# Score matmuls with the low query parts on 64 partitions, and the first head's operands made earlier

## Chip, cores and metric

One core of a Trainium2 chip runs the whole kernel. The metric is the device time of one execution in microseconds; three runs were timed, and one more execution was profiled.

## What is computed

One layer of a streaming encoder step for 1024 prompt frames and 64 sample frames of width 1024: a half-step SwiGLU, one input projection into [u | q | k | v], an S5 state-space mixer with a gated output (u), differential attention with four heads (q, k, v), an output projection, cross attention into 256 memory tokens, a second half-step SwiGLU and a final norm. The part that the change touches is the attention of the prompt, all in float32:

```python
s = einsum('bqhme,bkhme->bhmqk', q, k) * 64 ** -0.5     # two maps m of 64 dims per head
s = s - slope[h] * abs(qpos - kpos)                     # masked by chunks of 64
p = softmax(s)
w = p[:, :, 0] - lam * p[:, :, 1]
out = einsum('bhqk,bkhv->bqhv', w, v)
```

and, ahead of it, the gate of the state-space mixer, `y * sigmoid(y @ w_glu + b_glu)`.

## The kernel before

The whole step is written as one stream of Python that emits instructions; a scheduler of the framework orders the instructions of each engine by readiness and by their place in the program, gives out buffers and sets the waits. Rows of 128 x 1088 float32 come from one pool of 36 buffers (`row()`), PSUM banks from a pool of seven (`bank()`).

Float32 precision is had from the fast float32r form by splitting an operand x into a rounded high part and a low part x - high. A full product takes three matmuls (high x high, high x low, low x high), done by `mm3` (line 176) for the projections.

**The gating units** (lines 1683 to 1697). Four units f, one for each 128 columns of `w_glu`. `unit` (from line 190) issues 36 matmuls with `mm3`, ScalarE takes the sigmoid from PSUM (L1693), VectorE multiplies with y (L1695), and the product is stored to memory (L1697). It is loaded again at steps 32 to 35 of the attention loop (`Y_AT`). Before the matmuls of the last unit (f == 3) head 0 is set up: `head_start(0)` and `q_stack(heads[0], 6)`.

**Operands of a head.** `head_start` (line 1461) makes two key tiles `ks[m]` of 128 x 1024, one for each map m. The 64 partitions of map m (`hi_`) hold the high part of the keys, cast by ScalarE (L1471); the other 64 (`lo_`) hold the low part, made by GpSimd (L1472). It also loads the bias of the head on SP (L1474). `q_stack` (line 1481) does the same for 256 queries at a time, for both maps, in a tile [128, map, r, 256]: r = 0 holds the high part of the queries in both halves of the partitions (ScalarE L1488, GpSimd L1489), so that one matmul over 128 partitions with `ks[m]` gives q_high k_high + q_high k_low. r = 1 holds the low part of the queries in the half `hi_` (GpSimd L1490) and zeros in the other half (GpSimd L1491), so that a second matmul over 128 partitions adds q_low k_high.

**The attention loop** (from line 1708). 32 blocks of 128 queries, four heads with eight blocks each, in the order 7, 6, ..., 0 (`ORDER`); block i sees (i + 1) x 128 keys. Step n does the scores of block n, `combine` of block n - 2, `transposes` of block n - 4 and `values` of block n - 5 (`LAGS`). `scores` issues, for each map and each cut of the keys (one cut up to 512 keys, else two), the two matmuls at L1508 into one bank; VectorE adds the bias and takes the minimum out of PSUM (L1511), ScalarE takes the exponential (L1517). `combine` is VectorE work (L1525 to L1528), `transposes` go through TensorE (L138) and ScalarE (L1538), `values` are float32 matmuls (L1544, each in two records). At step 1 of each head `stream` adds the attention of the 64 sample frames into the cache as background work (its scores L1579, its values L1614, and two matmuls over 64 partitions, L1615). `q_ready(n + 2)` makes a query tile two steps ahead, and `head_start` of the next head is called at step 5 of a head (`HEAD_AT`). After the loop the memory projection follows (matmuls at L1761), whose weights are loaded and split in advance (L145, L162, L163).

The two matmuls for one bank, as they stand before:

```python
for r in range(2):
    T.matmul(p[:, :c1 - c0], s.qs[i // 2][:, m, r, (i % 2) * P:(i % 2 + 1) * P], s.ks[m][:, c0:c1],
             start=(r == 0), stop=(r == 1))
```

Of the kernel before, what the change touches and what calls it, by code (L numbers as in the profile page):

```python
# [10 lines left out]
F32 = mybir.dt.float32  # L11
# [6 lines left out]
P = 128  # L18
# [21 lines left out]
ORDER = (7, 6, 5, 4, 3, 2, 1, 0)  # L40
# [29 lines left out]
def tile_hymba_step(ctx: ExitStack, tc: tile.TileContext, a, o):  # L70
# [15 lines left out]
    V, A, G, T = nc.vector, nc.scalar, nc.gpsimd, nc.tensor  # L86
# [8 lines left out]
    def row(shape=(P, NT), dt=F32):  # L95
        return rows.tile(list(shape), dt, tag="r", name=nm("r"))

    def bank():
        return ps.tile([P, 512], F32, tag="b", name=nm("b"))

    def small(shape, tag, dt=F32):
        return sp.tile(list(shape), dt, tag=tag, name=nm(tag), bufs=6 if tag in ("rr", "ss", "mn", "xr") else 3)
# [89 lines left out]
    def unit(wsrc, xs, mid=None, chs=CHS):  # L192
        return units([wsrc], xs, mid, len(xs) // 2, chs)[0]

    def chunks(p, t):

        return [(pc[:, :c1 - c0], t[:, c0:c1]) for pc, (c0, c1) in zip(p, CHS)]
# [1266 lines left out]
    def head_start(hd):  # L1464

        s = Head()
        s.hd, s.k, s.q, s.v = hd, kT[hd], qT[hd], vt[hd]
        s.ks = [row([P, NP], F32R) for _ in range(2)]
        for m in range(2):
            lo_, hi_ = slice(64 * (1 - m), 64 * (1 - m) + 64), slice(64 * m, 64 * m + 64)  # L1470
            A.copy(s.ks[m][hi_], s.k[hi_, :NP])  # L1471
            G.tensor_tensor(out=s.ks[m][lo_], in0=s.k[hi_, :NP], in1=s.ks[m][hi_].bitcast(F32), op=ALU.subtract)  # L1472
        s.bias = row([P, NP])
        load(out=s.bias, in_=a["c_bias_p"][hd])  # L1474
        s.oh, s.hx = row([P, 8, P]), row([P, 4, P])
        s.ssq = small([P, 9], "ssq")
        s.qs = [None] * 4
        V.memset(s.ssq, 1.0)
        return s

    def q_stack(s, i):

        s.qs[i // 2] = row([P, 2, 2, 256], F32R)
        qs = s.qs[i // 2]
        c = slice(i * P, i * P + 256)
        for m in range(2):
            lo_, hi_ = slice(64 * (1 - m), 64 * (1 - m) + 64), slice(64 * m, 64 * m + 64)
            A.copy(qs[hi_, m, 0], s.q[hi_, c])  # L1488
            G.tensor_copy(qs[lo_, m, 0], s.q[hi_, c])  # L1489
            G.tensor_tensor(out=qs[hi_, m, 1], in0=s.q[hi_, c], in1=qs[hi_, m, 0].bitcast(F32), op=ALU.subtract)  # L1490
            G.memset(qs[lo_, m, 1].bitcast(F32), 0.0)  # L1491

    class Item:
        pass
# [1 line left out]
    def scores(s, i):  # L1496

        nk = (i + 1) * P
        it = Item()
        it.s, it.i, it.nk = s, i, nk  # L1500
        it.pm, it.ss, mn = [], small([P, 2], "ss"), small([P, 4], "mn")
        cut = [(0, max(nk, 256))] if nk <= 512 else [(0, nk // 256 * 128), (nk // 256 * 128, nk)]
        for m in range(2):
            w = row([P, NP])
            for j, (c0, c1) in enumerate(cut):
                p = bank()
                for r in range(2):
                    T.matmul(p[:, :c1 - c0], s.qs[i // 2][:, m, r, (i % 2) * P:(i % 2 + 1) * P], s.ks[m][:, c0:c1],  # L1508
                             start=(r == 0), stop=(r == 1))
                c1 = min(c1, nk)  # L1510
                V.tensor_tensor_reduce(out=w[:, c0:c1], in0=p[:, :c1 - c0],  # L1511
                                       in1=s.bias[:, NP - nk + c0:NP - nk + c1], scale=-0.125, scalar=BIG,
                                       op0=ALU.add, op1=ALU.min, accum_out=mn[:, 2 * m + j:2 * m + j + 1])
            if len(cut) == 2:
                V.tensor_tensor(out=mn[:, 2 * m:2 * m + 1], in0=mn[:, 2 * m:2 * m + 1],
                                in1=mn[:, 2 * m + 1:2 * m + 2], op=ALU.min)
            A.activation(w[:, :nk], w[:, :nk], AF.Exp, bias=mn[:, 2 * m:2 * m + 1], scale=-1.0,  # L1517
                         accum_out=it.ss[:, m:m + 1])
            it.pm.append(w)
        return it  # L1520
# [162 lines left out]
    heads, items = [None] * 4, []  # L1683
    ysp = [split(y.rearrange("p s c -> p (s c)")) for y in yT]
    wglu = a["w_glu"][0].rearrange("(k p) m -> p k m", p=P)
    for f in range(4):
        if f == 3:
            heads[0] = head_start(0)
            q_stack(heads[0], ORDER[0] - ORDER[0] % 2)
        p = unit(wglu[:, :, f * P:(f + 1) * P], ysp)  # L1690
        s = row()
        for pc, sc_ in chunks(p, s):
            A.activation(sc_, pc, AF.Sigmoid, bias=b_glu[f])  # L1693
        z = row()
        V.tensor_tensor(out=z.rearrange("p (c s) -> p s c", s=TS), in0=s.rearrange("p (s c) -> p s c", s=TS),  # L1695
                        in1=yT[f], op=ALU.mult)
        store(out=y_d[f], in_=z)  # L1697
# [3 lines left out]
    def q_ready(n):  # L1701

        hd, i = seq[n]
        if heads[hd].qs[i // 2] is None:
            q_stack(heads[hd], i - i % 2)

    q_ready(1)
    for n in range(32 + LAGS[2] + 1):
        if n < 32:
            if n % 8 == STREAM_AT:  # L1710
                bg.append(stream(heads[n // 8]))
            items.append(scores(heads[n // 8], seq[n][1]))
            if n % 8 == HEAD_AT and n < 24:
                heads[n // 8 + 1] = head_start(n // 8 + 1)
            if n < 30:
                q_ready(n + 2)
        if n == MEM_AT:
            bg.append(mem_norm())
        if n in Y_AT:
            y = row()  # L1720
            load(out=y, in_=y_d[Y_AT.index(n)])
            cat[Y_AT.index(n)] = y
        if 0 <= n - LAGS[1] < 32:
            transposes(items[n - LAGS[1]])
        if 0 <= n - LAGS[0] < 32:
            combine(items[n - LAGS[0]])
        pump_all()
        if 0 <= n - LAGS[2] < 32:
            m = n - LAGS[2]
            values(items[m])  # L1730
            items[m] = None
            if m % 8 == 7:
                bg.append(subln(heads[m // 8]))
# [334 lines left out]
```

## Time and profile before

| what | value |
|---|---|
| median of three runs | 2386.49 us (2383.15 to 2392.55) |
| the profiled execution | 2393.03 us, its span 2391.2 us |
| instructions | 45853 |
| TensorE busy | 2265.2 us, 95% of the span |
| VectorE busy | 1599.6 us, 67% |
| ScalarE busy | 1289.3 us, 54% |
| GpSimd busy | 1083.4 us, 45% |
| mean granted TensorE clock | 0.98 |

PE is TensorE's matmuls, PEld its weight loads, DVE VectorE, ACT ScalarE, POOL GpSimd, SP the queue that issues the loads and stores. L1508 is line 1508 of the kernel. Matmuls overlap each other, so the busy time of PE includes the filling and draining of the array; from the start of one matmul to the start of the next is what tells how fast it works. The granted clock PEclk is a share of 2.4 GHz.

### The profile page before, as it was taken

The page shows a single profiled execution, that of the slowest core. Times are in us where ns is not written, and L with a number is a line of the kernel's source. Part 1 is how long each engine was busy: PE and PEld are TensorE (multiplying, and loading weights), DVE is VectorE, ACT ScalarE, POOL GpSimd, SP SyncE. Part 2 cuts the span into 40 slices and gives each one's busy share as a digit, 9 for nine tenths or more (in the row PEclk, how much of TensorE's full clock was granted, in tenths as well). Part 3 has the DMA queues.
Part 4 walks back from the last instruction along what each step waited for, and adds up shares of the span by engine and source line. Part 5 has one row for each costly group of instructions (what it writes and reads, how often), then busy time and mean ns, then how long its engine had stood idle before and what let it go on. Part 6 is the DMA issues. An engine that isn't in the chain of part 4 may idle for free.

```text
span 2391.2 us, 45853 instructions
## 1 busy us (share of the span) xinstructions
PE 2265.2 (95%) x16914; PEld 2202.8 (92%) x16914; DVE 1599.6 (67%) x3318; ACT 1289.3 (54%) x2506; POOL 1083.4 (45%) x1048
## 2 busy tenths in 40 slices
PE   6999999998999898998999999898999999999998
PEld 6999999998999897997789999798899999999998
DVE  7666344336888688238988788788655555568897
ACT  6554445446554421237866766676544545466543
POOL 1567777882018704425510500024788886630050
PEclk9999999998999998999999999999999999999999
DMA  6232444678434647864336541152255452265422
GB/s 214 80 109 76 121 127 132 221 248 312 141 125 147 202 127 206 257 187 146 116 118 198 180 154 41 49 188 91 87 163 174 161 165 87 76 224 172 164 69 85
DMA packets 374316, 354.97 MB, mean 148 GB/s; under 512 B 42654, under 2 KB 313035, under 8 KB 374091
## 3 DMA queue, kind: packets, MB, share of 16 engines
q1 hardware_dynamic: 374000, 352.01, 46.5%
q8 instruction: 133, 2.18, 0.4%
q14 instruction: 93, 0.75, 0.1%
q10 hardware_dynamic: 90, 0.02, 0.0%
HBM read 245.23 MB, written 102.14 MB: 145 GB/s over the span
## 4 chain that ended last, share of the span: by engine, by line
PE 57%; DVE 14%; POOL 11%; DMA 8%; issue 4%; ACT 3%; SPq 1%; DVEq 0%; POOLq 0%; ACTq 0%
PE b L176 49%; PE b L138 2%; DMA r<-w_ffn_d 2%; PE b L1761 2%; DMA down_d<-r 2%; DMA wr<-w_ffn_gu 2%; DVE wl L154 2%; POOL r L715 1%; DVE r L419 1%; POOL wr L674 1%; PE b L1508 1%; POOL ws L675 1%; POOL ws L673 1%; POOL ws L672 1%; POOL r L702 1%
## 5 line engine op out<-in xcount | busy, mean ns | idle before, releaser
L176 PE MATMUL b<-r,wh 128*128 128x272 f32 (+4 forms) x9600 | 1690.8, 296 | 54.8 <-DVE r L783 15.1
L176 PEld LDWEIGHTS b<-r,wh 128*128 128x128 f32 x9600 | 1422.8, 191 | 71.1 <-DVE r L783 17.4
L176 PE MATMUL b<-r,wl 128*128 128x272 f32 (+4 forms) x4800 | 1058.3, 295 | 8.1 <-DVE wl L154 8.1
L176 PEld LDWEIGHTS b<-r,wl 128*128 128x128 f32 x4800 | 787.9, 191 | 10.2 <-DVE wl L154 9.9
L652 DVE TENSOR_TENSOR r<-b,r 128x272 f32<-128x272 f32 x440 | 172.0, 434 | 253.5 <-PE b L176 152.1
L153 ACT CAST q<-wr 128x512 fp32r<-128x512 f32 x280 | 166.2, 594 | 240.6 <-DVE wl L154 232.1
L154 DVE TENSOR_TENSOR wl<-wr,q 128x512 fp32r<-128x512 f32 x280 | 190.8, 681 | 147.9 <-issue 82.8
L152 ACT CAST wh<-wr 128x512 fp32r<-128x512 f32 x280 | 172.7, 621 | 193.3 <-PE b L176 189.0
L154 DVE TENSOR_TENSOR wl<-ws,q 128x512 fp32r<-128x512 f32 x206 | 140.5, 682 | 108.6 <-ACT q L153 70.0
L834 POOL TENSOR_TENSOR r<-r,r 128x544 f32<-128x544 f32 x40 | 64.6, 1621 | 321.0 <-DVE r L783 311.6
L419 DVE TENSOR_TENSOR r<-r,r 128x544 fp32r<-128x544 f32 x224 | 175.0, 799 | 36.9 <-ACT r L418 36.3
L153 ACT CAST q<-ws 128x512 fp32r<-128x512 f32 x206 | 121.8, 591 | 140.6 <-DVE wl L154 94.9
L152 ACT CAST wh<-ws 128x512 fp32r<-128x512 f32 x206 | 127.5, 621 | 123.1 <-PE b L176 96.8
L593 POOL TENSOR_TENSOR r<-r,r 128x544 f32<-128x544 f32 x28 | 43.6, 1559 | 280.1 <-ACT r L592 279.4
L418 ACT CAST r<-r 128x544 fp32r<-128x544 f32 x224 | 144.5, 649 | 22.9 <-DMA r<-hid_d 22.6
L783 DVE SCALAR_TENSOR_TENSOR r<-b,r 128x272 f32<-128x272 f32 (+4 forms) x328 | 133.3, 441 | 34.8 <-PE b L176 28.9
L672 POOL TENSOR_TENSOR ws<-wr,wr 128x512 f32<-128x512 f32 x44 | 61.4, 1395 | 138.3 <-DMA wr<-w_ffn_gu 128.1
L138 PE MATMUL b<-ident,r 128*128 128x128 f32 (+4 forms) x649 | 94.7, 283 | 24.0 <-DMA r<-g_subln 9.9
L715 POOL TENSOR_TENSOR r<-r,r 128x1088 f32<-128x1088 f32 x44 | 112.0, 2545 | 9.4 <-ACT r L714 9.4
L138 PEld LDWEIGHTS b<-ident,r 128*128 128x128 f32 (+4 forms) x649 | 76.2, 145 | 36.1 <-DMA r<-x_prompt 9.9
L446 POOL TENSOR_TENSOR ws<-ws 128x128 f32<-128x128 f32 x48 | 32.5, 678 | 150.6 <-DVE r L1269 63.7
L153 ACT CAST q<-r 128x512 fp32r<-128x512 f32 x90 | 53.0, 588 | 86.8 <-DVE wl L154 86.8
(348 smaller groups left out, 2950.2 us busy)
## 6 DMA issues: line engine op xcount, KB each, us to landing
wr<-w_ffn_gu SPq DMA_DIRECT2D x194, 256.0 KB, 3.0
r<-w_ffn_d SPq DMA_DIRECT2D x100, 256.0 KB, 4.4
hid_d<-r SPq DMA_DIRECT2D x44, 544.0 KB, 2.8
r<-hid_d SPq DMA_DIRECT2D x44, 544.0 KB, 6.2
down_d<-r SPq DMA_DIRECT2D x40, 512.0 KB, 4.0
h_d<-r SPq DMA_DIRECT2D x48, 272.0 KB, 2.4
r<-h_d SPq DMA_DIRECT2D x48, 272.0 KB, 4.0
sums_d<-ws SPq DMA_DIRECT2D x48, 256.0 KB, 3.1
```

Of the source, the lines that this page charges most:

```text
L138: T.transpose(out, in_, ident[:n, :n])
L152: A.copy(hi, x)
L153: A.copy(r, x)
L154: V.tensor_tensor(out=lo, in0=x, in1=r.bitcast(F32), op=ALU.subtract)
L176: T.matmul(pc[:, :c1 - c0], w, x[:, c0:c1], start=(first + i == 0 and q == 0), stop=(first + i == n - 1 and q == 2))
L418: A.copy(r[:, 0], v)
L419: V.tensor_tensor(out=r[:, 1], in0=v, in1=r[:, 0].bitcast(F32), op=ALU.subtract)
L652: V.tensor_tensor(out=oc, in0=pc, in1=tc_, op=ALU.add)
L672: G.tensor_tensor(out=s1, in0=r[2], in1=r[3], op=ALU.add)
L715: G.tensor_tensor(out=up, in0=up, in1=gate, op=ALU.mult)
L783: V.scalar_tensor_tensor(out=hc_, in0=pc, scalar=0.5, in1=hc_, op0=ALU.mult, op1=ALU.add)
L834: (V if n_ else G).tensor_tensor(out=o_, in0=o_, in1=x_, op=ALU.add)
```

## The change

Three edits. The low part of the queries is multiplied over the 64 partitions of its map alone, with the same 64 partitions of the key tile, so that the zeros in the other half of r = 1 are neither written nor read. `head_start(0)` is called before the second gating unit (f == 1) instead of the last. The two query tiles of head 0 that the first blocks need are made before the third unit (queries 768 to 1023) and before the fourth (512 to 767); before, only the first of them was made there.

```diff
             G.tensor_tensor(out=qs[hi_, m, 1], in0=s.q[hi_, c], in1=qs[hi_, m, 0].bitcast(F32), op=ALU.subtract)
-            G.memset(qs[lo_, m, 1].bitcast(F32), 0.0)
...
                 p = bank()
-                for r in range(2):
-                    T.matmul(p[:, :c1 - c0], s.qs[i // 2][:, m, r, (i % 2) * P:(i % 2 + 1) * P], s.ks[m][:, c0:c1],
-                             start=(r == 0), stop=(r == 1))
+                qs, hi_ = s.qs[i // 2][:, m, :, (i % 2) * P:(i % 2 + 1) * P], slice(64 * m, 64 * m + 64)
+                T.matmul(p[:, :c1 - c0], qs[:, 0], s.ks[m][:, c0:c1], start=True, stop=False)
+                T.matmul(p[:, :c1 - c0], qs[hi_, 1], s.ks[m][hi_, c0:c1], start=False, stop=True)
...
     for f in range(4):
-        if f == 3:
+        if f == 1:
             heads[0] = head_start(0)
-            q_stack(heads[0], ORDER[0] - ORDER[0] % 2)
+        if f > 1:
+            q_stack(heads[0], (f == 2) * 2 + 4)
         p = unit(wglu[:, :, f * P:(f + 1) * P], ysp)
```

## Rows read from the trace of the kernel before

**Rows 1.** The page, part 1: busy us, share of the span, instructions.
```profile
PE 2265.2 (95%) x16914; PEld 2202.8 (92%) x16914; DVE 1599.6 (67%) x3318; ACT 1289.3 (54%) x2506; POOL 1083.4 (45%) x1048
```

**Rows 2.** The chain of waits at the attention's start: start us, us, what.
```profile
1080.53 0.93 ACT r L1471
...
1081.53 3.44 POOL r L1472
...
1085.05 2.36 POOL r L1472
...
1087.45 1.16 PE b L1508 x4
...
1088.62 2.42 POOL r L1490
```

**Rows 3.** Windows of 4 us: length, busy us of each engine, clock, DMA share, GB/s.
```profile
core 0: us, PE busy (x) PEld busy (x) DVE busy (x) ACT busy (x) POOL busy (x), PEclk, DMA share, GB/s
...
1064.00:1068.00 4.00, 4.00 (x26) 4.00 (x25) 1.47 (x2) 0.00 (x0) 0.00 (x0) 1.00 0.00 0
...
1092.00:1096.00 4.00, 2.57 (x7) 1.78 (x7) 3.99 (x16) 3.48 (x6) 1.61 (x5) 0.50 1.04 280
```

**Rows 4.** Windows over the attention stage, with the same columns.
```profile
1085.00:1100.00 15.00, 11.04 (x38) 8.57 (x38) 13.02 (x29) 8.97 (x18) 10.61 (x15) 0.66 0.60 168
1100.00:1140.00 40.00, 37.41 (x245) 30.68 (x244) 37.56 (x135) 33.25 (x78) 19.24 (x33) 1.00 0.34 103
1140.00:1180.00 40.00, 37.28 (x265) 31.98 (x263) 37.19 (x130) 32.22 (x78) 21.53 (x30) 1.00 0.35 105
1180.00:1220.00 40.00, 37.03 (x257) 30.93 (x257) 39.32 (x144) 34.60 (x83) 20.01 (x29) 1.00 0.36 111
1220.00:1243.00 23.00, 23.00 (x184) 21.07 (x184) 16.64 (x67) 15.31 (x42) 2.32 (x2) 1.00 0.46 145
```

**Rows 5.** TensorE in order of time, 1109 to 1131: start us, us, instructions.
```profile
1121.17 1.62 PE L1508 MATMUL b<-r,r 128*128 128x512 f32 x6
...
1122.63 1.58 PE L138 MATMUL b<-ident,r 128*128 128x128 f32 x13
...
1127.13 3.74 PE L1614 MATMUL b<-r,r 128*128 128x128 f32 x32
```

**Rows 6.** TensorE's groups, 1085 to 1243.2: busy us, mean ns, idle before; L1508 by source line.
```profile
L138 PE MATMUL b<-ident,r 128*128 128x128 f32 x312 | 43.9, 280 | 4.1 <-DVE r L1545 3.0 <-DVE r L1528 0.7
L1544 PE MATMUL b<-r,r 128*128 128x128 f32 x287 | 38.7, 279 | 0.9 <-DVE mn L1511 0.9
...
L1579 PE MATMUL b<-r,r 128*128 128x512 f32 x32 | 15.1, 595 | 0.0
...
L1508 PE MATMUL b<-r,r x192: 278/363/796, 1085.0 to 1228.9; 128*128 128x384 f32 x80, 128*128 128x512 f32 x64, 128*128 128x256 f32 x48
```

**Rows 7.** GpSimd by source line: ns min/median/max; who waited for L1491 (us, times).
```profile
L1491 POOL MEMSET r<- x32: 304/307/312, 1059.0 to 1215.1; 64x256 f32 x32
...
PEld b L1508: 0.2, 1
...
L1472 POOL TENSOR_TENSOR r<-r,r x8: 2347/2710/3445, 1081.5 to 1185.8; 64x1024 fp32r<-64x1024 f32 x8
```

**Rows 8.** TensorE in order of time, 1130.1 to 1131.5: start us, us.
```profile
1129.92 0.94 PE L1614 MATMUL b<-r,r 128*128 128x128 f32 x7
1130.80 0.48 PE L1615 MATMUL b<-r,r 64*128 64x128 f32 x2
1131.21 0.49 PE L1544 MATMUL b<-r,r 128*128 128x128 f32 x2
```

**Rows 9.** TensorE in order of time, 209.9 to 211.2, in the first SwiGLU.
```profile
210.00 0.41 PE L176 MATMUL b<-r,wl 128*128 128x272 f32 x2
210.35 0.33 PE L138 MATMUL b<-ident,r 64*128 64x64 f32 x2
210.61 0.77 PE L176 MATMUL b<-r,wh 128*128 128x272 f32 x4
```

## Prediction

> **What bounds the kernel now.** I read the page's busy shares first, then the chain of waits around the edited lines, then windows of the attention stage, and last the order of single instructions on TensorE. The shares say that TensorE is the engine to watch over the whole run [rows 1], but a share is an average, and the change touches one stage only: the attention, which runs from the first score matmul at 1085 us to the first matmul of the memory projection at about 1243 us, 158 us.
>
> The chain shows what holds the start of that stage. ScalarE makes the two key tiles of head 0 (L1471), GpSimd their low halves (L1472, two of them, one after the other), and TensorE gets its next score matmuls at 1087.45 when the second is done. It runs out again and waits for the low part of the queries (L1490) until 1088.62 + 2.42 = 1091.04 [rows 2]. These two waits are 2.36 and 2.42 us. The windows show the price: in the four us from 1092 TensorE has 2.57 us busy and the granted clock is 0.50, its lower level of 1.2 GHz, after the idle pieces before it. They also show room beforehand: from 1064 to 1068 TensorE is full with the gating units while ScalarE, GpSimd and the DMA stand at 0.00 [rows 3].
>
> From 1100 to 1220 VectorE is the fullest engine: 37.56, 37.19 and 39.32 of 40 us, together 114.1 of 120, or 95%. TensorE shows 37.41, 37.28 and 37.03 [rows 4]. But a busy matmul of the profile includes its fill and drain, so I count TensorE's work by spacing instead. Six score matmuls of 512 columns take 1.62 us; less one duration of some 0.40 that is 0.244 us from start to start. In runs of 128-column float32 matmuls the spacing is (3.74 - 0.28) / 31 = 0.112 us, of transposes (1.58 - 0.28) / 12 = 0.108 us [rows 5]. With the counts of the stage [rows 6]: 192 score matmuls of 395 columns on average (64 of 512, 80 of 384, 48 of 256) at 0.244 x 395 / 512 = 0.188 us are 36 us; 320 transposes x 0.108 are 35; 288 value matmuls x 0.112 are 32; the stream's four runs of 32 x 0.112 are 14, and its scores 15 by their busy time; 2 more for the small ones. Together 134 of 158 us. So VectorE sets the pace and TensorE has 24 us to spare, a part of it before 1100, where it is busy for only 11.04 of 15 us [rows 4].
>
> **Part one: low products on 64 partitions.** It removes 32 memsets of 0.307 us on GpSimd, 9.8 us. I cost them at nothing: only one score matmul waited for one, for 0.2 us [rows 7], and GpSimd is busy for 45% of the span [rows 1]. The number of matmuls stays at 192 with the same columns. Half of them, 96, now use 64 rows of the array.
>
> Does a matmul of 64 rows take less? The stream has the pair to compare: matmuls of 128 columns with 128 rows (L1614) and then with 64 (L1615). The two of L1615 last 0.48 us together, no less than two of the other kind [rows 8]. So nothing is saved by the smaller contraction.
>
> Does going from one form to the other cost? The last of L1614 ends at 1129.92 + 0.94 = 1130.86, the two of L1615 end at 1131.28: 0.42 us for two matmuls that at 0.112 would be 0.22. So 0.20 us are lost on entering the form with 64 rows. The next two with 128 rows end at 1131.70: again 0.42 for 0.22, so 0.20 us on the way back [rows 8]. The same in the first stage, where the neighbours are of the float32r kind of the scores: the return is 211.38 - 210.68 = 0.70 us for four matmuls spaced about 0.12, a loss of 0.22; the entry is 0.27 us for two of 64 columns, which at half of the 0.112 would be 0.11, a loss of 0.16 [rows 9]. I take 0.19 us a switch. The next weights are evidently not loaded under the running matmul there.
>
> In the change every low product stands between two products of 128 rows: high, low, high, low, one pair for each bank. That is 96 entries and 96 returns, 192 x 0.19 = 36.5 us more on TensorE in this stage. By the lowest reading (0.16 in, 0.20 out) it is 35 us, by the highest (0.20, 0.22) 40. The bound below is zero, if a matmul that stood after a wait anyway hides it.
>
> Here the trace and a rule can be weighed. L1615 took as long with 64 rows as L1614 with 128 [rows 8]. The Trainium skill's page TensorEngine Tiling (Array Packing) gives, under Theoretical Speedup, up to twice the speed for a contraction of at most 64, and, under Key Properties, a drain of TensorE where the tiling mode changes. By the first rule alone the sum would fall by half of the low products' time; by the second it would grow, since here a product of full height stands between any two low ones. The rows of this trace side with the second, and it is they that give the price.
>
> **Part two: operands made earlier.** The two casts of L1471 (about 1 us each), the two subtractions of L1472 (2.7 us each [rows 7]) and the bias load of head 0 go from before the last gating unit to before the second. The query tiles of head 0 for rows 4 to 7 go before the third and fourth: four casts on ScalarE, four on GpSimd, four subtractions. They are covered by the gating units' matmuls, beside which lie four us where those engines and the DMA are empty [rows 3]. On SP the bias load moves ahead of some loads of memory-projection weights that no matmul needs before 1243. On GpSimd nothing else is queued until the attention. What moves with it is a collision: while L1472 runs, VectorE's work beside it stretches; that will now fall on the products of a gating unit, which go to memory and are read only behind the scores. If the cover were gone, the 5.4 us of GpSimd would stand where they stand now. So the part takes away the waits of 2.36 and 2.42 us [rows 2] and perhaps the clock's fall: 5 us, at most some 7.
>
> **The sum.** TensorE's work in the stage becomes 134 + 36.5 = 171 us, VectorE's stays at about 144 (13.0 + 114.1 + 16.6). So TensorE becomes the bound. Without one idle moment the stage takes 171, which is 13 us more than now. With the full price on top of today's path it would be 36.5 more. If the bounding engine is kept 95% busy, as VectorE is now, it is 171 / 0.95 = 180 us, 22 us more; the waits at the start that part two removes are inside this figure, since it counts them as work that flows. The profiled execution took 2393.03 us for a span of 2391.2, 6.5 us above the median of 2386.49; the difference goes on the median: 2386.5 + 22 = 2408 us.
>
> **The rivals.** *Not slower:* VectorE keeps the pace. The place is the queue of seven banks between score matmuls and L1511; if it stays filled, a drained TensorE costs nothing, and part two's 5 us are left: 2381 us. It decides if the switches fall where TensorE waits anyway, so up to its 24 spare us. Against it: 36.5 is more than 24, and much of the 24 lies in the start. Chance 0.08. *Half hidden:* the order of instructions, which a scheduler makes, changes and puts low products side by side, or the slack takes most: 0 to 12 us more, 2388 to 2398. Chance 0.13. *All on the path:* waits between TensorE and VectorE do not shrink, because each bank now comes later: 29 to 37 us more, 2415 to 2424. Chance 0.15. *The clock falls:* the pieces in which the array drains bring the clock of 0.50 [rows 3] back for 12 us in each head; with TensorE's work at 85%, that is up to 10 us a head, 2424 to 2450. For it: it fell at the start. Against: it stayed at 1.00 from 1100 to 1243 through idle pieces [rows 4]. Chance 0.03. *The 64 rows halve the low products:* they run in half the time, 96 x 0.188 / 2 = 9 us, and no switch costs anything; with part two's 5 us that makes 14 less, 2372, if VectorE can follow. Against it are the 0.48 us that the two matmuls of 64 rows lasted [rows 8]. Chance 0.03. This is what Theoretical Speedup of the page TensorEngine Tiling (Array Packing) in the Trainium skill would do here; the trace does not agree.
>
> **How the numbers follow.** The forecast has 0.58: 2398 to 2415, from TensorE without idle to a little under 95% packing. With the half hidden and the all-on-path cases the range 2388 to 2424 holds 0.86. Some 0.5%, or 12 us, is what a measurement of this kernel tells from no change. Slower by over that: 0.58 + 0.15 + 0.03, rounded down to 0.75 since the forecast's lower end lies on the border. Within it: 0.22. Faster: 0.03.
>
> **What would show it.** Right: L1508 appears with 64*128 matmuls, 96 of them; in a burst of scores the spacing rises by about 0.19; weight loads show an idle piece of about 0.1 us before each; VectorE's share from 1100 on falls under 90% and its idle time is ended by L1508; the first score matmuls come at about 1085 without waits for L1472 or L1490. Wrong: the spacing of a pair stays near 0.4 us (the price is not paid), or the stage stays at 158 us although it is (VectorE hid it), or the clock leaves 1.00 in mid-stage.

## The result, and the profile after

The changed kernel takes 2427.89 us (median of four runs, 2424.41 to 2429.0) where the kernel before takes 2388.63 us (four runs, 2383.15 to 2392.55): a ratio of 1.0156, 95% interval [1.0139, 1.0174]. It is slower, by 37 to 39 us instead of the forecast 22, and lies 4 us above the top of the range. The profiled execution took 2428.95 us for a span of 2427.2. Of the 36.0 us between the two profiled spans, 31.4 lie in the attention stage, 4.1 ahead of it and 0.6 behind it.

The page of the kernel after, part 1 (busy us, share, instructions) and the granted clock in 40 slices:

```profile
PE 2302.5 (95%) x16914; PEld 2211.2 (91%) x16914; DVE 1604.4 (66%) x3318; ACT 1289.8 (53%) x2506; POOL 1080.6 (45%) x1016
...
PEclk9999999998999998997999999999999999999999
```

Against [rows 1] TensorE gains 37 us of busy matmuls and 8 of weight loads; VectorE, ScalarE and GpSimd stay within 5 us. The slice with a 7 is the start of the attention. The shares tell no more than that, so the stage itself is next. Windows over the attention stage after (columns as in [rows 4]); the stage now runs from the first score matmul at 1089.1 to the first matmul of the memory projection at 1278.7, 189.6 us instead of 158.2:

```profile
core 0: us, PE busy (x) PEld busy (x) DVE busy (x) ACT busy (x) POOL busy (x), PEclk, DMA share, GB/s
1089.00:1094.00 5.00, 4.83 (x14) 2.13 (x12) 4.04 (x6) 2.49 (x6) 4.73 (x5) 1.00 0.85 264
1094.00:1111.00 17.00, 17.00 (x34) 8.58 (x34) 10.19 (x42) 7.92 (x14) 4.24 (x9) 0.51 0.44 139
1111.00:1115.00 4.00, 2.23 (x6) 0.80 (x4) 3.32 (x11) 3.95 (x11) 1.46 (x2) 0.93 0.00 0
1115.00:1125.00 10.00, 9.47 (x30) 7.01 (x31) 7.34 (x16) 7.17 (x14) 4.08 (x2) 0.50 0.15 54
1125.00:1165.00 40.00, 40.00 (x233) 29.22 (x232) 30.93 (x105) 24.48 (x60) 12.80 (x19) 1.00 0.32 93
1165.00:1205.00 40.00, 38.13 (x216) 27.96 (x213) 31.40 (x111) 26.40 (x64) 14.74 (x18) 0.96 0.28 81
1205.00:1245.00 40.00, 38.12 (x238) 28.77 (x237) 35.69 (x128) 29.26 (x69) 17.53 (x18) 1.00 0.34 106
```

Two things differ from [rows 4]. From 1125 on VectorE falls from 95% to (30.93 + 31.40 + 35.69) / 120 = 82%: it waits, and TensorE sets the pace. And from 1094 to 1125 the granted clock stands at its lower level of 1.2 GHz for two stretches, 17 and 10 us; a third of 3.4 us lies near 1197 (the 0.96). The first begins while TensorE is busy with alternating score matmuls, the second in an idle piece of 2.3 us. In all it is 30.7 us of the stage, against 10.2 in the profile of before.

TensorE in order of time at full clock, after (start us, us, instructions): the pairs of 512 columns, and those of 384:

```profile
1142.76 0.50 PE L1507 MATMUL b<-r,r 128*128 128x512 f32 x1
1143.19 0.49 PE L1508 MATMUL b<-r,r 64*128 64x512 f32 x1
1143.62 0.55 PE L138 MATMUL b<-ident,r 128*128 128x128 f32 x3
...
1149.35 0.44 PE L1508 MATMUL b<-r,r 64*128 64x384 f32 x1
1149.72 0.44 PE L1507 MATMUL b<-r,r 128*128 128x384 f32 x1
1150.09 0.44 PE L1508 MATMUL b<-r,r 64*128 64x384 f32 x1
```

From start to start 512 columns now take 0.43 us where the burst of [rows 5] had 0.244, and 384 take 0.37 where the same rate gives 0.183: 0.19 us more at each change of the row count, in both directions. The same pairs where the clock is halved, from the chain of waits after (start us, us, what):

```profile
1093.92 0.43 PE b L1508
1094.35 0.62 PE b L1507
1094.97 0.62 PE b L1508
1095.59 0.72 PE b L1507
1096.31 0.72 PE b L1508
```

There 384 columns take 0.62 and 512 take 0.72, so a slow stretch adds 0.25 to 0.29 us to each score matmul. What the weight loads and VectorE wait for, by source line L1508 of after (us, times):

```profile
its engine sat idle before it (us, times) until:
  issue: 15.4, 66
...
who waited for it (us, times):
  DVE r L1510: 14.0, 34
```

Before 66 of the 96 weight loads of the low products the profile shows an idle piece, 15.4 / 66 = 0.23 us in the mean, with nothing that they wait for. VectorE's scores (L1510, L1511 before) wait 14.0 us for the low products. In order of time each load now starts together with its matmul and no longer under the one before (weight loads after, full clock and half clock):

```profile
1149.35 0.18 PEld L1508 LDWEIGHTS b<-r,r 64*128 64x128 f32 x1 [0.19 <-issue]
...
1098.81 0.28 PEld L1508 LDWEIGHTS b<-r,r 64*128 64x128 f32 x1 [0.33 <-issue]
```

The load takes 0.18 us where a change costs 0.19. In the slow stretch it takes 0.28, and a change there costs 0.62 less 0.32, the spacing of three neighbours of 384 columns at half clock in the kernel before (1095.36, 1095.68, 1096.00): 0.30. So the price is about one weight load that is no longer hidden; no run tells this apart from the emptying of the array itself.

The operands of head 0, after, ScalarE in order of time (start us, us, instructions):

```profile
1075.26 1.47 ACT L1693 ACTIVATE r<-b,gc 128x364 f32<-128x364 f32 x3
1076.61 2.12 ACT L1471 CAST r<-r 64x1024 fp32r<-64x1024 f32 x2
...
1080.63 0.82 ACT L1488 CAST r<-r 64x256 fp32r<-64x256 f32 x2
```

and GpSimd in the same stretch (in brackets its idle time before, and what ended it):

```profile
1077.79 6.19 POOL L1472 TENSOR_TENSOR r<-r,r 64x1024 fp32r<-64x1024 f32 x2 [32.12 <-PE b L176]
1084.04 3.00 POOL L1489 CAST r<-r 64x256 fp32r<-64x256 f32 x2
1087.11 3.65 POOL L1490 TENSOR_TENSOR r<-r,r 64x256 fp32r<-64x256 f32 x2
```

The casts of L1471 don't run in the empty windows of [rows 3]: on ScalarE they stand behind a weight cast, ahead of which it idles 5.5 us for L176's matmuls, and behind the three sigmoids of the first gating unit (L1693). GpSimd starts L1472 at 1077.8, then must do L1489, whose two casts now take 3.00 us, and makes the low queries last, until 1090.76. In the kernel before, L1489 had been done long before, at 0.39 us a cast. What stretches it isn't shown. Two lines of before (GpSimd, then TensorE's weight loads) and two of after (TensorE):

```profile
1058.67 0.39 POOL L1489 CAST r<-r 64x256 fp32r<-64x256 f32 x1 [16.69 <-PE b L138]
...
1088.59 1.06 PEld L1508 LDWEIGHTS b<-r,r 128*128 128x128 f32 x4 [0.21 <-POOL r L1490]
...
1089.11 0.40 PE L1507 MATMUL b<-r,r 128*128 128x512 f32 x1
1089.67 0.49 PE L1508 MATMUL b<-r,r 64*128 64x512 f32 x1 [0.17 <-POOL r L1490]
```

So the waits at the start did go: the first low product came 3.6 us behind the first score matmul (1085.02) before, and 0.6 us behind it now. The first score matmul itself comes right behind the last gating matmul in both kernels. (Everything in this run, already ahead of the first edited instruction, is 4 us later than in the profile of before; the first sigmoid starts at 1075.3 instead of 1071.0.)

Behind the stage, SP's order has changed. The four loads at L666 in the second SwiGLU, before and after, in the order of time of SP's queue:

```profile
1665.90 2.11 SPq L666 DMA_DIRECT2D r<-w_ffn_gu  x4
...
1706.44 2.15 SPq L666 DMA_DIRECT2D r<-w_ffn_gu  x4
```

and the waits of TensorE's weight loads, before from 1655 to 1740 and after from 1688 to 1775 (us in total, times, longest):

```profile
PEld b L176 <- ACT wh L152: 1.6, 1, 1.6
...
PEld b L176 <- ACT wh L152: 5.7, 3, 3.4
```

In the kernel before these loads leave 0.4 us ahead of the transposes of `rhy` that begin this stretch; now they leave 6.3 us behind them (at 1700.19), since a load of L145 that waits for a free buffer has come to stand ahead of them on the queue.

### The profile page after: what moved, and what is told of

It is laid out like the page before. It is cut to its first block, busy times and chain, and to the rows that moved or that the text cites. A ratio compares the mean times of both kernels' runs of the same rounds, so it can differ in the third digit from the quotient of the medians.

```text
span 2427.2 us, 45818 instructions
## 1 busy us (share of the span) xinstructions
PE 2302.5 (95%) x16914; PEld 2211.2 (91%) x16914; DVE 1604.4 (66%) x3318; ACT 1289.8 (53%) x2506; POOL 1080.6 (45%) x1016
## 4 chain that ended last, share of the span: by engine, by line
PE 67%; DVE 11%; DMA 7%; POOL 6%; issue 4%; ACT 3%; SPq 1%; DVEq 0%; POOLq 0%; ACTq 0%
PE b L176 56%; PE b L138 3%; PE b L1761 2%; DVE wl L154 1%; PE b L1508 1%; DMA down_d<-r 1%; DMA r<-w_ffn_d 1%; PE b L1507 1%; PE b L1543 1%; DMA wr<-w_ffn_gu 1%; DVE r L419 1%; PE b L1578 1%; PE b L1613 1%; POOL r L834 1%; POOL r L702 1%
## 5 line engine op out<-in xcount | busy, mean ns | idle before, releaser
L176 PE MATMUL b<-r,wh 128*128 128x272 f32 (+4 forms) x9600 | 1691.4, 296 | 54.4 <-DVE r L783 15.3
L176 PEld LDWEIGHTS b<-r,wh 128*128 128x128 f32 x9600 | 1424.1, 191 | 70.2 <-DVE r L783 17.3
L176 PE MATMUL b<-r,wl 128*128 128x272 f32 (+4 forms) x4800 | 1058.5, 295 | 8.4 <-DVE wl L154 8.3
L176 PEld LDWEIGHTS b<-r,wl 128*128 128x128 f32 x4800 | 786.9, 191 | 10.6 <-DVE wl L154 10.4
L418 ACT CAST r<-r 128x544 fp32r<-128x544 f32 x224 | 144.2, 649 | 22.7 <-DMA r<-hid_d 22.5
```

Source lines behind the costliest of these rows:

```text
L176: T.matmul(pc[:, :c1 - c0], w, x[:, c0:c1], start=(first + i == 0 and q == 0), stop=(first + i == n - 1 and q == 2))
L418: A.copy(r[:, 0], v)
```

## The experiments

All were run with the kernel before on the same chip beside them; its median was 2394.6 to 2397.1 us there, so ratios are compared, not times. Diffs are against the kernel after. In the table the stage is again first score matmul to first memory matmul, "changes" are the changes of row count between neighbouring matmuls in it, "to 37th" is the time from the first score matmul to the start of the 37th (the first four blocks have 32, the fifth four), "half clock" the time in the stage at the lower clock, "behind" the rest of the span. Stage, half clock and "behind" come from one profile of each run.

| run | stage us | changes | to 37th us | half clock us | behind us | ratio, interval |
|---|---|---|---|---|---|---|
| before | 158.2 | 14 | 21.5 | 10.2 | 1147.9 | |
| after | 189.6 | 192 | 29.8 | 30.7 | 1148.5 | 1.0156 [1.0139, 1.0174] |
| base | 158.5 | 14 | 21.8 | 6.8 | 1142.3 | |
| p1_low64_only | 184.0 | 174 | 26.3 | 20.5 | 1152.5 | 1.0104 [1.0079, 1.0130] |
| p2_early_only | 155.0 | 14 | 19.6 | 0 | 1151.2 | 1.0013 [1.0000, 1.0026] |
| low64_grouped | 181.3 | 166 | 27.0 | 17.1 | 1152.7 | 1.0120 [1.0102, 1.0138] |
| low64_heads123 | 174.9 | 144 | 19.9 | 0 | 1154.1 | 1.0109 [1.0092, 1.0127] |
| early_tail | 158.0 | 14 | 22.4 | 6.8 | 1144.2 | 0.9989 [0.9978, 1.0001] |
| low64_tail | 187.1 | 186 | 30.9 | 23.9 | 1143.5 | 1.0115 [1.0097, 1.0134] |
| low64_grouped2 | 158.7 | 78 | 19.6 | 10.2 | 1148.7 | 1.0002 [0.9988, 1.0017] |
| low64_late_tail | 179.0 | 162 | 22.7 | 6.8 | 1146.9 | 1.0080 [1.0052, 1.0108] |
| low64_first4_tail | 162.8 | 38 | 28.3 | 20.5 | 1140.2 | 1.0012 [0.9995, 1.0029] |
| early_mid | 156.2 | 14 | 21.1 | 3.4 | 1145.0 | 0.9994 [0.9980, 1.0008] |
| low64_grouped_mid | 159.3 | 80 | 20.4 | 10.2 | 1146.1 | 0.9998 [0.9985, 1.0012] |

### One part at a time

The low products on 64 rows alone; the operands where they were:

```diff
-        if f == 1:
+        if f == 3:
             heads[0] = head_start(0)
-        if f > 1:
-            q_stack(heads[0], (f == 2) * 2 + 4)
+            q_stack(heads[0], ORDER[0] - ORDER[0] % 2)
```

> Part one alone: low products on 64 partitions, head 0 made where it was before. Theory S (192 changes between 128 and 64 rows at 0.20 us each, and a clock that falls in the drained stretch): slower than before by 34 to 42 us, so as slow as the whole change or up to 5 us slower. Rival P (the early operands cost the time): within 4 us of before. Rival L (a matmul of 64 rows is itself slow): 34 to 42 us as well.

The early operands alone; the low products with zeros on 128 rows:

```diff
+            G.memset(qs[lo_, m, 1].bitcast(F32), 0.0)
...
-                T.matmul(p[:, :c1 - c0], qs[:, 0], s.ks[m][:, c0:c1], start=True, stop=False)
-                T.matmul(p[:, :c1 - c0], qs[hi_, 1], s.ks[m][hi_, c0:c1], start=False, stop=True)
+                for r in range(2):
+                    T.matmul(p[:, :c1 - c0], s.qs[i // 2][:, m, r, (i % 2) * P:(i % 2 + 1) * P], s.ks[m][:, c0:c1],
+                             start=(r == 0), stop=(r == 1))
```

> Part two alone: head 0's operands early, the low products over 128 partitions with zeros as before. Theory S: 3 to 6 us faster than before, first score matmuls without a wait for L1472 or L1490, and a clock that stays at 1.00 around 1090 to 1100 us. Rival P: 30 us or more slower. A third outcome, within 2 us of before, would say that the waits at the start were hidden by VectorE anyway.

Part one alone makes the stage 25.8 us longer. As a whole it is 25 us slower (1.0104), so the early operands don't cause the loss, but the 34 to 42 us of both other theories were too many. Part two alone makes the stage 3.2 us shorter, with the clock at 1.00 throughout. Yet it is not the 3 to 6 us faster as a whole that theory S had: its rest is longer, and the wait behind the stage is there again (waits of the weight loads, 1650 to 1740, p2_early_only):

```profile
PEld b L176 <- ACT wh L152: 6.5, 2, 4.9
```

### Is it the change of the row count or the 64 rows?

Four high products of a block, then its four low ones, written in that order:

```diff
+        for (m, j), p in banks.items():
+            c0, c1 = cut[j]
+            T.matmul(p[:, :c1 - c0], qs[m][:, 0], s.ks[m][:, c0:c1], start=True, stop=False)
+        for (m, j), p in banks.items():
+            c0, c1 = cut[j]
+            hi_ = slice(64 * m, 64 * m + 64)
+            T.matmul(p[:, :c1 - c0], qs[m][hi_, 1], s.ks[m][hi_, c0:c1], start=False, stop=True)
```

> As the change, but each block issues its two or four high products one after the other and then its low products: 64 changes of rows in place of 192, the same matmuls. Theory S: 128 changes fewer at 0.20 us are 25.6 us, so 0 to 8 us slower than before. Rival L (the 64-row matmul is slow in itself): as slow as the change, 35 to 40 us. If low products on rows 0 to 63 and 64 to 127 that follow each other run side by side, up to 9 us less than theory S, so down to 8 us faster than before.

This run told nothing of grouping: the scheduler put most products back in pairs, and 166 changes were left. So the order was fixed by edges that carry no semaphore, each low product behind the one before it:

```diff
+            low = T.matmul(p[:, :c1 - c0], qs[m][hi_, 1], s.ks[m][hi_, c0:c1], start=False, stop=True)
+            tc.add_manual_dep(low.ins, last.ins.name, mybir.DependencyInfo(
+                mybir.DependencyClass.NoSync, mybir.DependencyReason.DATA), reason="low products behind the high ones")
+            last = low
```

> As the change, with edges that keep the order: in each block all high products, then all low products, so 64 changes of rows in place of 192; the loads behind the attention are in their order of before. Theory S (only the change of rows costs, 0.20 us each): TensorE's work is 134 + 13 = 147 us, under VectorE's, and the stage takes 153 to 163 us: 5 us faster to 5 us slower than before. Rival L (a matmul over 64 rows is itself slow): 25 us or more slower. If neighbours on rows 0 to 63 and 64 to 127 run side by side, the spacing of low products falls from about 0.19 to 0.1 us.

With the same 96 products on 64 rows but 78 changes, the whole loss is gone: stage 158.7, ratio 1.0002. So the 64 rows alone don't cost it; the changes of the row count do. (The edit does one thing more: the low products of the two maps now run side by side, last section. By the prediction's 0.188 us for each that saves 48 x 0.188 = 9 us of TensorE's work, an estimate, where 114 changes fewer save 114 x 0.19 = 22.) Windows of low64_grouped2 show VectorE as the fullest engine in the sum again, at 37.02, 36.95 and 39.25 of 40 us, as in [rows 4]:

```profile
1094.40:1134.40 40.00, 35.51 (x239) 27.24 (x237) 37.02 (x120) 31.76 (x77) 15.04 (x19) 1.00 0.31 92
1134.40:1174.40 40.00, 38.11 (x268) 30.05 (x266) 36.95 (x135) 32.98 (x78) 20.57 (x22) 1.00 0.36 107
1174.40:1214.40 40.00, 37.78 (x255) 28.89 (x255) 39.25 (x143) 34.42 (x83) 18.71 (x20) 1.00 0.35 108
```

### Is it the clock at the start?

Head 0 keeps zeros and 128 rows; the other three heads have 64:

```diff
+            if s.hd == 0:
+                G.memset(qs[lo_, m, 1].bitcast(F32), 0.0)
...
+                if s.hd == 0:
+                    hi_ = slice(0, P)
```

> As the change, but head 0 keeps zeros and 128 rows: 144 changes of rows in place of 192, and none in the first 40 us of the stage. Theory S (some 9 us of the loss are the half clock at the start): 12 to 18 us slower than before, the clock 1.00 at the start. Rival U (only the number of changes counts, the clock takes little): three quarters of the loss of the change, 25 to 29 us slower.

The clock stays up for the whole stage (windows of low64_heads123):

```profile
1090.00:1105.00 15.00, 12.83 (x50) 7.36 (x48) 13.99 (x48) 8.87 (x16) 10.33 (x19) 1.00 0.76 246
1105.00:1125.00 20.00, 15.97 (x109) 12.97 (x109) 18.74 (x58) 19.57 (x49) 10.69 (x11) 1.00 0.29 79
1125.00:1165.00 40.00, 39.11 (x229) 28.65 (x229) 32.47 (x110) 26.85 (x62) 16.88 (x20) 1.00 0.32 94
```

It gives the net price at full clock: (174.9 - 158.5) / (144 - 14) = 0.126 us for each added change against base, and (174.9 - 155.0) / 130 = 0.153 against p2_early_only, which has the same early operands and no half clock either. That is two thirds to four fifths of the 0.19; the rest goes into time that TensorE had to spare. From either base the 178 added changes of the kernel after make a stage of 181 to 182 us, and it took 189.6. The other 7 to 9 us should then be the clock. As a whole, though, the run is 26 us slower, the 25 to 29 of rival U and not the 12 to 18 of theory S: its stage, 16 us longer, is as S has it, and the rest lies behind the stage (next section). Two runs split the same question at the first four blocks of head 0, both with SP's later order kept (next section). All but the first four blocks on 64 rows, and the first four alone (here `not (...)` in both places):

```diff
+            if s.hd == 0 and i > 3:
+                G.memset(qs[lo_, m, 1].bitcast(F32), 0.0)
...
+                if s.hd == 0 and i > 3:
+                    hi_ = slice(0, P)
```

> 64 rows for the low products everywhere but in the first four score blocks of head 0, which keep the zeros and 128 rows (160 row changes on the score matmuls where the change has 192); the first head's operands are made early, and SyncE's later loads stand in the order of the kernel before. Theory: a row change costs 0.11 us net at full clock, as the run without 64 rows in head 0 showed (16.4 us for 144), and the rest of the change's 31 us is the clock, which falls because the stage begins with drained matmuls: here the start is undrained, the clock stays at 1.00 over the first 30 us, the stage takes 176 to 178 us and the total is 0.7 to 0.9% above before. Rival: the loss is even over the changes, whatever the start does (28.6 us for 186 in the run with 64 rows everywhere and this order): 160 changes give 24 to 25 us, a stage of 182 to 184 us and a total 1.0 to 1.1% above, with the half clock at the stage's start as before.

> 64 rows for the low products only in the first four score blocks of head 0 (32 row changes); all other blocks keep the zeros and 128 rows; operands early, SyncE's later loads in the order of before. Theory that the drained start lets the clock fall: half clock for 10 us or more within the first 30 us of the stage, and a stage 8 to 13 us over the 158 us of before (32 x 0.11 = 3.5 for the changes and the rest for the clock), total 0.3 to 0.5% above. Rival, that the loss is even over the changes: 32 x 0.15 = 5 us, a stage of 160 to 163 us, total within 0.2% of before.

The first came out nearer to the clock theory: 179.0 us, 1 us above its range and 3 below the rival's, no long slow stretch, 0.8% over before (the interval reaches the rival's 1.0%). Its 6.8 us of half clock lie in two pieces at the same places as in early_tail, from which it differs only by the 64 rows behind the fourth block: (179.0 - 158.0) / 148 = 0.142 us a change at the same clock. By that price the kernel after would take 183 us, so 6 to 9 us in all are left for the clock. (The texts reckoned with 0.11 for a change, not taking off the 14 that are there before; with 0.126 to 0.153 they would have said 177 to 178.) The second agrees with it on the clock, half clock for 17 us six us into the stage (windows of low64_first4_tail):

```profile
1096.00:1102.00 6.00, 4.57 (x16) 2.40 (x14) 5.13 (x10) 2.33 (x6) 5.63 (x6) 1.00 0.89 297
1102.00:1119.00 17.00, 17.00 (x34) 8.85 (x34) 10.10 (x42) 10.01 (x18) 5.28 (x13) 0.51 0.33 109
...
1123.00:1258.80 135.80, 130.41 (x928) 113.47 (x926) 121.95 (x443) 108.46 (x261) 59.06 (x84) 0.99 0.38 115
```

but on the time it sides with the even loss, 162.8 us and 0.12%. The column "to 37th" settles where it lies. Putting the first four blocks on 64 rows makes that part 5.9 us longer alone (28.3 against early_tail's 22.4) and 8.2 us longer beside the other blocks (low64_tail's 30.9 against low64_late_tail's 22.7). The rest of the stage is the same with and without it, within 1.1 us. The edit adds 24 changes. At the full 0.19 they are 4.6 us, at the net 0.126 they are 3.0, so between 1.3 and 5.2 us are left for the clock, an estimate, since no run changes the clock alone. So the long fall at the start comes with 64 rows in the first blocks, and its price there is below the 6 to 9 us. The kernel after has another slow stretch of 10 us behind the first and a stage 2.5 us longer than low64_tail's; how the 6 to 9 us divide isn't settled.

### What was lost behind the stage?

In the kernel after, p1_low64_only, p2_early_only, low64_grouped and low64_heads123 some loads late on SP stand in another order than before. In the next two kernels the operands are still early, but both query stacks are made before the last unit, and SP's order behind the attention is that of the kernel before:

```diff
-        if f > 1:
-            q_stack(heads[0], (f == 2) * 2 + 4)
+        if f == 3:
+            q_stack(heads[0], 6)
+            q_stack(heads[0], 4)
```

With zeros and 128 rows, and with 64 rows; beside them the kernel before again, as "base":

> Part two alone in another form: head 0 set up before the second gating unit, both query tiles made before the fourth, zeros and 128 rows as before. Here the loads on SP and the work on GpSimd behind the attention stand in the same order as before the change, which they do not in p2_early_only. Theory T (the scheduler's new order of later loads takes back what the early operands give): stage about 155 us, nothing lost behind it, 2 to 5 us faster than before. Rival (the loss behind the stage has another cause): 1 to 4 us slower, like p2_early_only.

> The whole change, but with both query tiles of head 0 made before the fourth gating unit, which leaves the loads on SP behind the attention in their order of before; in the change one load of the second SwiGLU's weights stands ahead of four others. Theory T: the stage as in the change, 184 to 190 us, and some 6 us less than the change behind it: 26 to 34 us slower than before. Rival: as slow as the change, 36 to 40 us.

> The kernel before, profiled once more beside the others. All theories: a stage of 157 to 160 us with some 10 us at half clock. Theory T: from the stage's end to the end of the span 1145 to 1149 us. If that is 1151 us or more, the 5 us that the variants lose there are the chip's and not the scheduler's.

The long wait is gone (weight loads from 1680 to 1770, low64_tail):

```profile
PEld b L176 <- ACT wh L152: 1.8, 2, 1.6
```

It is 1.6 us before, 1.8 in low64_tail and 0.5 in low64_late_tail, where SP has its old order, and 5.7, 6.5, 6.2 and 6.2 us in after, p2_early_only, low64_grouped and low64_heads123, where these loads come late. (p1_low64_only has an order of its own and waits 1.9 us here; where its long rest comes from was not looked into.) Behind the stage the nine profiles with the old order took 1140.2 to 1148.7 us, the five with a new one 1148.5 to 1154.1: 1145 and 1152 in the mean. The scatter is nearly as large: the kernel before took 1147.9 and, as base, 1142.3, under the 1145 to 1149 that were expected. Counted along TensorE's matmuls, the same in all runs, the loss lies in one place: from the 3001st behind the stage to the 3501st the nine take 72.9 to 73.8 us, the four with the load ahead of L666 80.5 to 82.0, p1_low64_only 74.8. So the new order costs 7 to 8 us there, of which the longer wait for the cast weights explains 4 to 5; what the others wait for was not traced. The two main profiles hide it, 1147.9 and 1148.5 behind the stage, since the rest of the kernel before happened to be slow elsewhere.

The early operands alone bring little: early_tail's stage is 158.0 us and not the 155 of its theory. It is 2.6 us faster as a whole, within the theory's 2 to 5, but the interval holds 1. low64_tail is 27.6 us slower, as theory T had it (26 to 34).

### Is there a version that beats both?

All of head 0's operands before the third unit, so the queries one unit earlier than in early_tail and the keys one unit later; zeros and 128 rows, SP's order kept:

```diff
-        if f == 1:
+        if f == 2:
             heads[0] = head_start(0)
-        if f > 1:
-            q_stack(heads[0], (f == 2) * 2 + 4)
+        if f == 2:
+            q_stack(heads[0], 6)
+        if f == 2:
+            q_stack(heads[0], 4)
```

> The low products as before (zeros, 128 rows); the first head's normalisation and both its stacks of queries are made beside the second gating unit, one stage step earlier than in the run that kept SyncE's order, with SyncE's later loads still in the order of before. Theory: the early operands are worth 3 us at the stage's start (155.0 us in the run that had them alone) and what that run lost behind the stage came from SyncE's changed order, so here the stage takes 155 to 156 us, the stretch behind it as much as before, and the total is 0.9975 to 0.999 of before. Rival: the start is bound by the keys' transfers and VectorE whatever is made early, and the stage takes 158 us as in the run with the order kept: 0.999 to 1.001.

and the same with the grouped low products of low64_grouped2:

> 64 rows for the low products with the four high products of a block ahead of its four low ones (64 score changes of row count instead of 192), and the first head's operands made one step earlier than in the change's last step, beside the gating unit's third part, so that SyncE's order is that of before: the change in the best form that the runs so far point to. Theory: VectorE bounds the stage (it is busy for 142.9 of 158.7 us in the grouped run), so TensorE's saved low products buy nothing beyond the 2 us that the earlier operands gave; stage 155 to 158 us, total 0.998 to 1.001 of before. Rival: the side-by-side low products and GpSimd's 48 dropped zero fills now count, stage 150 to 154 us, total 0.996 to 0.998. Third: the grouped changes still let the clock fall at the stage's start, stage 158 to 161 us, total 1.000 to 1.002.

Neither can be told from the kernel before (0.9994 and 0.9998, both intervals hold 1). early_mid's stage is 2 us shorter, as its theory had it, but nothing of the size forecast for the total can be shown. In low64_grouped_mid the third case held for the stage: 159.3 us with 10.2 us of half clock at its start. (Its text speaks of 48 zero fills; there are 32 [rows 7].) No run was faster than before beyond its interval.

## Why the prediction was wrong in its size and right in its main mechanism

**The switch.** Right. 0.19 us was taken from [rows 8] and [rows 9], and 0.19 is what a score matmul of either size pays in each direction. The Trainium skill's page TensorEngine Tiling (Array Packing), under Key Properties, has TensorE drain where the tiling mode changes; the trace agrees that the change costs, 0.19 us at full clock with these weights of 128 columns, but not whether it is the drain or the weight load behind it.

**What of it lies on the path.** Nearly right at full clock. The forecast had a stage of 180 us, 22 more, for TensorE as the bound; the net prices of 0.126 to 0.153 us give 181 to 183, 22 to 25 more. The 95% was borrowed from VectorE and somewhat high: by the same sum low64_heads123 has 134 + 130 x 0.19 = 159 us of TensorE's work in a stage of 174.9, 91%. VectorE fell to 82% (forecast: under 90%), its waits are ended by L1508, and the weight loads show an idle piece, 0.23 us instead of "about 0.1".

**Part two.** Right in the waits, wrong in their worth. The two waits went, as forecast, and the gating units did cover the work. But the step "beside which lie four us where those engines and the DMA are empty" has no part in it: the casts can't use those four us, since a cast that waits and the sigmoids of the first unit stand ahead of them on ScalarE, and L1489 went from long done to standing behind L1472 on GpSimd. The forecast took 5 us for the two waits. Alone, part two gave 3.2 us in the stage, 0.2 in early_tail and 2.0 in early_mid; beside part one it gave nothing, 189.6 us against the 184.0 of p1_low64_only, with 18 more changes and 10 us more of half clock.

**The clock.** Here is the first step that failed: the sentence that part two takes away "perhaps the clock's fall", with a chance of 0.03 for the rival. With part two alone the clock did stay at 1.00 in p2_early_only; early_tail and early_mid still had 6.8 and 3.4 us of half clock, as base had 6.8. With the alternating products in the first blocks it fell for 17 us and again for 10. The rival had the thing right that happened and the place wrong: not in each head but where the stage begins, and in mid-stage for 3.4 us alone. It was dismissed because of idle pieces later in the stage that left the clock up [rows 4], but the stage's first blocks, where the clock had fallen before [rows 3], were the place to look at. Its price is at most the 6 to 9 us by which the stage grew beyond what the changes cost at full clock; 1.3 to 5.2 us of it are left for the first four blocks.

**The missing term.** The second failed step is "On SP the bias load moves ahead of some loads of memory-projection weights that no matmul needs before 1243". The sum ended with the stage, although moving an earlier load changed the scheduler's order of later ones too. A load waiting for a buffer came ahead of four loads of the second SwiGLU, and TensorE waited 5.7 us there instead of 1.6; the stretch takes 7 us more. It is enough to decide whether the time lies in the range: low64_tail, the whole change without it, has a ratio of 1.0115, which on 2388.63 is 2416 us.

**The halving rival.** As the change was written it fell with 0 us gained. The grouped run shows that it holds where low products of the two maps stand next to each other (last section); there the 9 us saved about pay for the 64 added changes (64 x 0.126 to 0.153 is 8 to 10 us), and VectorE sets the pace again.

**The range.** 2388 to 2424 held the forecast and the all-on-path case but no sum of the two missing terms: 22 to 25 for the changes and the 6 to 9 left for the clock, together the stage's 31.4, and 7 behind the stage are 38, within the 37 to 39 that were measured.

## What to carry to other kernels

Price a smaller contraction by the neighbours in the final instruction order: one that stands between full ones cost two changes of 0.19 us here and saved nothing, the same ones side by side paid for theirs (a stage of 158.7 us against 158.5). Moving work earlier in the program moves it only as far as what stands ahead of it on its engine lets it, so look that up; and compare the order of the load queue to the end of the kernel, not to the end of the stage. Where a stage starts with an engine whose clock has fallen there before, count added changes in those first blocks dearer than in the rest (here 5.9 to 8.2 us for 24, where the rest paid 0.126 to 0.153 each).

## What the runs showed that was not expected

*Two half matmuls run at once.* TensorE of low64_grouped2 in order of time, two maps of a block with 256 keys:

```profile
1141.95 0.48 PE L1506 MATMUL b<-r,r 128*128 128x256 f32 x2
1142.36 0.39 PE L1510 MATMUL b<-r,r 64*128 64x256 f32 x2
1142.67 0.87 PE L138 MATMUL b<-ident,r 128*128 128x128 f32 x6
```

The two low products, one on partitions 0 to 63 and one on 64 to 127, take 0.39 us together, about what a single one takes in the kernel after (0.38); their starts in the trace are 1142.359 and 1142.362. The Trainium skill's page TensorE: Matmul & The Clock Gate, in Part 3, says that matmuls on distinct groups of rows run concurrently with starts about 4 ns apart; the trace agrees, 3 ns here and 2 to 9 in the run's other pairs; only the first block's low products don't pair up so.

*A busy TensorE at the lower clock.* In the window 1094 to 1111 of the kernel after the profile shows it busy for 17.00 of 17 us with the granted clock at 0.51, and in the 5 us before it fell for 4.83 of 5. What the busy time hides is seen in the spacing: 384 columns from start to start in 0.62 us there and in 0.37 at full clock. The runs with 64 rows alternating in the first four blocks had 17.1 to 30.7 us of half clock in the stage, those with 128 rows there 0 to 10.2, and the two grouped ones 10.2 each, no more than before. What sets the fall off beyond that isn't shown.
